# Small experts: the down projection in plain float32, with the unsplit weights as the stationary operand

## The chip, the cores and the metric

The kernel runs on one core of one Trainium2 chip. Its time is the device time of one execution in microseconds; runs are compared by their median. Besides the timed runs there is one execution taken with the hardware profiler; all rows below come from that.

## The reference

A two-layer encoder on 256 tokens of width 1024 in float32. Layer 0 ends in a dense SwiGLU, layer 1 in a mixture of eight SwiGLU experts of inner width 3584, of which each token uses two:

```python
logits = (t @ w_router).astype(jnp.float32)
top_v, top_i = lax.top_k(logits, TOP_K)
gates = jax.nn.softmax(top_v, axis=-1)
combine = jnp.sum(jax.nn.one_hot(top_i, N_EXPERTS) * gates[..., None], axis=1)
for e in range(N_EXPERTS):
    out = out + combine[:, e:e + 1] * (silu(t @ wg[e]) * (t @ wu[e])) @ wd[e]
```

Around it stand mixers, cross-attention and norms, which the change does not touch. The expert weights are 352 MB of float32, read once.

## The kernel before

**Numbers.** A float32 value is held as two parts of the type float32r, a rounded upper part and the rest, and a product is made of two or three matmuls of parts. Weights come from memory as float32 pieces of 1 MB (`raw`, 128 partitions of 2048 values). ACT copies the upper part (`wh`, L121, in two halves), DVE subtracts it for the lower part (`wl`, L123, whole piece), and PE multiplies by both. There are three buffers for `wh` and `wl`, and eleven for `raw`, taken in turn; a raw buffer is free for the next load when DVE has read it.

**Experts.** The loop runs over eight places; the experts are put into them by their number of tokens. Places 2, 4 and 7 (`SMALL`) have room for 64 tokens (`SCAP`), the others for 128. In a large place the tokens' upper and lower parts are separate tiles and a weight piece takes twelve matmuls (`mm3`). In a small place the 64 upper and the 64 lower columns stand side by side in one stationary tile of 128, and a piece takes eight matmuls of 512 columns (`mm2`, L994): four with `wh`, four with `wl`. The upper and lower halves of such a result are then added by the matmul that turns it.

**Chunks.** The inner width is cut into chunks of 1024, 1024, 1024 and 512. For a chunk, `gate_up` multiplies the tokens by eight pieces of gate and up weights (four for the last chunk) into `gu`. ACT scales the result out (`sgs`, L1026). `to_hT` turns it with PE: eight matmuls per 512 values, with `sgs` as the 128x128 plain-float32 weights and the 64 columns of `twice`, two stacked unit matrices, as the moving operand (L1047). ACT makes Silu of the gate part (L1049), DVE multiplies by the up part (L1050), and both split the product into upper and lower columns of `hs` (L129, L130). `hs` has two homes of one buffer each, the tags `hs` and `gain`, for the first and the second 512 values. `down` multiplies it by the pieces of down weights (four a chunk, two for the last) into two PSUM banks `y` that add up over the whole expert.

**Order.** The code asks for the down projection of a chunk after the gate and up of the next one: `gate_up(c)`, `down(c-1)`, `to_hT(c)`. The order of the instructions on each engine is fixed when the program is built; a scheduler moves them from the order of the code by its own estimate of when operands are ready. Each engine then works off its list strictly, and waits at an instruction whose operands or buffer are not ready. All weight loads are issued from SP's queue in the order of the code.

After the expert's last chunk the banks `y` are split (`split_y`), and `scatter` multiplies them by a one-hot matrix `st` and adds them to the rows of `x`. The last place's down projection stands behind the loop and is followed by the last norm (`finish`).

Of the kernel before, what the change touches and what calls it, by code (L numbers as in the profile page):

```python
# [55 lines left out]
def trunk_kernel(ctx: ExitStack, tc: tile.TileContext, io, out, stop=None):  # L56
# [716 lines left out]
    with ExitStack() as moe:  # L773
# [5 lines left out]
        def mbank(shape, name="mm"):  # L779
            return trp.tile(shape, F32, tag="tr", name=name)  # L780
# [133 lines left out]
        def slots(dst, t, e):  # L914

            at = byp[:, t, e:e + 1] if ids[1] is not None else pos[:, t, e:e + 1]
            chain["DVE"] = nc.vector.tensor_scalar(dst, iota2 if e in SMALL else iota, at, None, op0=OP.is_equal)

        def gained(kk, e, n, src):

# [34 lines left out]
        wg, wu, wd = io["moe_w_gate"][0], io["moe_w_up"][0], io["moe_w_down"][0]  # L955
        nch = len(CHUNKS)

        def one_hot(e):
            se = m2.tile([P, 2, P], F32, tag="sg", name="so", bufs=1)
            for t in range(2):  # L960
                slots(se[:, t, :], t, e)
            return se
# [8 lines left out]
            return rs  # L971

        def slots_T(e):
            se = one_hot(e)
            tp = mbank([P, 2, P], "setp")
# [3 lines left out]
            nc.scalar.activation(st, tp, AF.Copy)  # L979
            return st  # L980

        def gate_piece(w, e, c, i):

# [49 lines left out]

        def down_piece(e, c, i, parts=1):
            f0 = CHUNKS[c][0] + i * 256
            return load_w(wd[ids[e], f0:f0 + 256, :].rearrange("(k p) n -> p k n", p=P), 2, D, parts)

        def to_hT(e, sg, homes):
            hT = []
            for j, (pool, tag) in zip(range(sg.shape[-2]), homes):  # L1040
                hs = pool.tile([P, 2, 4, P], F32R, tag=tag, name="hs")
                if e in SMALL:

                    tp = mbank([P, 2, 4, SCAP], "htp")
# [3 lines left out]
                    h = m2.tile([P, 4, SCAP], F32, tag="hsm", name="hsm", bufs=1)
                    nc.scalar.activation(h, tp[:, 0, :, :], AF.Silu)  # L1049
                    nc.vector.tensor_tensor(h, h, tp[:, 1, :, :], op=OP.mult)  # L1050
                    hh = hs[:, 0, :, :]
                    chain["hh"], chain["hl"] = split_to(hh[:, :, 0:SCAP], hh[:, :, SCAP:P], h)
                    hT.append((hh, None))
                    continue
                tp = mbank([P, 4, P], "htp")
                for k in range(4):
                    nc.tensor.transpose(tp[:, k, :], sg[:, j, k * P:(k + 1) * P], ident)
                hh, hl = hs[:, 0, :, :], hs[:, 1, :, :]
                chain["hh"], chain["hl"] = split_to(hh, hl, tp)
                hT.append((hh, hl))  # L1060
            return hT

        def down(c, hT, yacc, i, w2):

            hh, hl = hT[i // 2]
            wh, wl = w2
            first, last = c == i == 0, c == nch - 1 and i == CHUNKS[c][1] // 256 - 1
            kn = [(i % 2 * 2 + k, k, n) for n in range(2) for k in range(2)]
            if hl is None:
                return mm2([(yacc[n], hh[:, kk, :], wh[:, k, n * 512:(n + 1) * 512], wl[:, k, n * 512:(n + 1) * 512])  # L1070
                            for kk, k, n in kn], first, last)
            return mm3([(yacc[n], hh[:, kk, :], hl[:, kk, :], wh[:, k, n * 512:(n + 1) * 512],
                         wl[:, k, n * 512:(n + 1) * 512]) for kk, k, n in kn], False, first, last)

        def split_y(yacc, n, pool=mA, tag="y"):
            y = pool.tile([P, 2, 512], F32R, tag=tag, name="y")
            split_to(y[:, 0, :], y[:, 1, :], yacc[n])
# [49 lines left out]
        twice = mA.tile([P, SCAP], F32, tag="twice", name="twice")  # L1127
        for i in range(2):
            nc.gpsimd.tensor_copy(twice[i * SCAP:(i + 1) * SCAP, :], ident[i * SCAP:(i + 1) * SCAP, i * SCAP:(i + 1) * SCAP])
        prev = y = st = nrs = pyacc = gf = None  # L1130
        for e in range(NE):
            for c in range(nch):
# [39 lines left out]
                        pyacc = nacc  # L1172
                        y = split_y(pyacc, 0)
                if c == 0:
                    yacc = [mmp.tile([P, 512], F32, tag="mm", name=f"y{n}") for n in range(2)]
# [133 lines left out]
```

## Time and profile before

| what | us |
|---|---|
| median of 3 runs (1668.41 to 1675.79) | 1669.49 |
| the profiled execution | 1665.06 |
| its span, first to last instruction | 1663.4 |
| expert loop, first gate/up matmul to the end | 638.7 to 1663.4 |

The span is the profiled part of the execution; 1.7 us lie around it. Each engine has its own line: PE is TensorE's matmuls, PEld its weight loads, DVE VectorE, ACT ScalarE, POOL GpSimd, SP the queue that issues the loads. A matmul's recorded duration overlaps the next one's, so PE's rate is read from starts. A plain-float32 matmul of the program is recorded as two matmuls and two weight loads; the type column says f32 for both kinds.

### The profile page before, as it was taken

What the parts mean: (1) busy time and instruction counts of PE and PEld (TensorE: products, weight loads), DVE (VectorE), ACT (ScalarE), POOL (GpSimd) and SP (SyncE); (2) the same over time, 40 slices, a digit from 0 to 9 for tenths busy, and PEclk for the clock granted to TensorE, in tenths of its full rate; (3) what the DMA queues carried; (4) which work ended last, traced back from release to release, by engine and by line L of the source; (5) the groups of instructions that cost most, each with busy time, mean ns of one, the idle gap of its engine ahead of it and who ended that gap; (6) DMA issues with size and microseconds to landing.
All of it is one profiled execution on the core that took longest, in us unless ns stands there. A gap on an engine that the chain in (4) does not pass through costs nothing. (4 is left out here: it accounts for less than half of the span.)

```text
span 1663.4 us, 22408 instructions
## 1 busy us (share of the span) xinstructions
PE 1572.4 (95%) x8448; PEld 1310.2 (79%) x8448; DVE 1262.8 (76%) x1214; ACT 1074.4 (65%) x1396; POOL 47.1 (3%) x75
## 2 busy tenths in 40 slices
PE   8999999999999999999999889999889999999885
PEld 7799889999989887888887667777667777777653
DVE  6785655445576657899988988978888978988876
ACT  6555554344554446787777787767777767677775
POOL 1010010000000102000000000000000000000000
PEclk9999999999999999999999999999999999999998
DMA  7456466565535586899999999999999999999980
GB/s 237 163 178 214 145 217 201 177 200 180 191 127 178 187 333 245 322 341 354 360 369 361 345 358 339 338 338 375 345 363 345 340 337 347 329 351 345 358 309 28
DMA packets 175409, 464.50 MB, mean 279 GB/s; under 512 B 9074, under 2 KB 64390, under 8 KB 175164
## 3 DMA queue, kind: packets, MB, share of 16 engines
q1 hardware_dynamic: 174412, 459.80, 77.0%
q0 software_dynamic: 880, 3.19, 0.6%
q8 instruction: 68, 1.11, 0.3%
q14 instruction: 49, 0.40, 0.1%
HBM read 461.90 MB, written 2.11 MB: 279 GB/s over the span
## 5 line engine op out<-in xcount | busy, mean ns | idle before, releaser
L123 DVE TENSOR_TENSOR wl<-raw,wh 128x2048 fp32r<-128x2048 f32 (+1 forms) x527 | 983.0, 1894 | 238.0 <-ACT wh L121 235.7
L121 ACT ACTIVATE wh<-raw 128x1024 fp32r<-128x1024 f32 x866 | 852.7, 1049 | 277.1 <-PE pws L141 92.0
L138 PE MATMUL gu<-wh,ch 128*128 128x512 f32 x560 | 221.3, 396 | 2.8 <-ACT sg L1030 2.8
L141 PE MATMUL gu<-wh,cl 128*128 128x512 f32 x560 | 219.7, 393 | 0.0
L144 PE MATMUL gu<-wl,ch 128*128 128x512 f32 x560 | 152.8, 395 | 10.6 <-DVE wl L123 10.5
L138 PE MATMUL pws<-nh,wh 128*128 128x256 f32 x560 | 137.5, 283 | 0.0
L141 PE MATMUL pws<-nl,wh 128*128 128x256 f32 x560 | 137.4, 283 | 0.0
L144 PEld LDWEIGHTS gu<-wl,ch 128*128 128x128 f32 x560 | 103.5, 188 | 40.3 <-DVE wl L123 19.1
L138 PEld LDWEIGHTS gu<-wh,ch 128*128 128x128 f32 x560 | 105.5, 188 | 27.1 <-ACT sg L1030 2.9
L994 PE MATMUL gu<-wl,ch 128*128 128x512 f32 x336 | 99.8, 419 | 24.5 <-DVE wl L123 23.5
L141 PEld LDWEIGHTS gu<-wh,cl 128*128 128x128 f32 x560 | 105.6, 189 | 21.8 <-DVE cl L1111 0.4
L141 PE MATMUL y<-wh,hs 128*128 128x512 f32 x280 | 110.9, 396 | 0.0
L138 PE MATMUL y<-wh,hs 128*128 128x512 f32 x280 | 110.4, 394 | 0.0
L138 PEld LDWEIGHTS pws<-nh,wh 128*128 128x128 f32 x560 | 106.2, 190 | 1.3 <-ACT wh L121 0.9
L141 PEld LDWEIGHTS pws<-nl,wh 128*128 128x128 f32 x560 | 106.0, 189 | 0.4
L994 PEld LDWEIGHTS gu<-wl,ch 128*128 128x128 f32 x336 | 59.0, 191 | 55.1 <-DVE wl L123 45.9
L994 PE MATMUL gu<-wh,ch 128*128 128x512 f32 x336 | 97.7, 405 | 4.4 <-ACT wh L121 4.3
L138 PE MATMUL acc<-wh,ch 128*128 128x512 f32 x216 | 84.7, 392 | 0.0
L141 PE MATMUL acc<-wh,cl 128*128 128x512 f32 x216 | 84.4, 391 | 0.0
L994 PEld LDWEIGHTS gu<-wh,ch 128*128 128x128 f32 x336 | 63.3, 192 | 24.1 <-ACT wh L121 10.8
L144 PE MATMUL y<-wl,hs 128*128 128x512 f32 x280 | 79.1, 404 | 2.0 <-DVE wl L123 2.0
L144 PE MATMUL pws<-nh,wl 128*128 128x256 f32 x560 | 78.9, 283 | 0.0
(363 smaller groups left out, 2182.2 us busy)
## 6 DMA issues: line engine op xcount, KB each, us to landing
raw<-in_moe_w_up_dram SPq DMA_DIRECT2D x112, 1024.0 KB, 6.5
raw<-in_moe_w_gate_dram SPq DMA_DIRECT2D x112, 1024.0 KB, 6.4
raw<-in_moe_w_down_dram SPq DMA_DIRECT2D x110, 1024.0 KB, 6.2
raw<-in_mem_w_kv_dram SPq DMA_DIRECT2D x16, 1024.0 KB, 5.5
raw<-in_odd_w_in_dram SPq DMA_DIRECT2D x12, 1024.0 KB, 5.3
raw<-in_ffn_w_gate_dram SPq DMA_DIRECT2D x11, 1024.0 KB, 5.1
raw<-in_ffn_w_up_dram SPq DMA_DIRECT2D x11, 1024.0 KB, 5.2
raw<-in_ffn_w_down_dram SPq DMA_DIRECT2D x11, 1024.0 KB, 4.7
```

The lines of the kernel that those rows point to most:

```text
L121: chain["wh"] = nc.scalar.activation(hf[:, sl], rf[:, sl], AF.Copy)
L123: chain["wl"] = nc.vector.tensor_sub(lf[:, sl], rf[:, sl], hf[:, sl].bitcast(F32))
L138: mm = nc.tensor.matmul(ps, ah, bh, start=f, stop=False, skip_group_check=bank)
L141: nc.tensor.matmul(ps, *((ah, bl) if w_left else (al, bh)), start=False, stop=False, skip_group_check=bank)
L144: mm = nc.tensor.matmul(ps, *((al, bh) if w_left else (ah, bl)), start=False, stop=e, skip_group_check=bank)
L994: mm = nc.tensor.matmul(ps, a, b[which], start=f, stop=e)
```

## The change

For the small places the weights of the down projection are no longer split: `down_piece` loads the raw piece alone, and `down` uses its 128x128 blocks as plain-float32 weights, with the hidden values as the 64 moving columns. The result is y transposed, eight blocks of 128 rows by 64 tokens in one PSUM bank. `to_hT` writes the hidden values as one float32 tile in the same two homes, without a split. `split_y` copies the bank once an expert (ACT, `yT`), turns it back with PE, four transposes for each half of the width, and splits that. One-hot tiles of a small place get 64 columns. Raw buffers of down pieces are now free when PE has used them.

```diff
         def down_piece(e, c, i, parts=1):
             f0 = CHUNKS[c][0] + i * 256
-            return load_w(wd[ids[e], f0:f0 + 256, :].rearrange("(k p) n -> p k n", p=P), 2, D, parts)
+            src = wd[ids[e], f0:f0 + 256, :].rearrange("(k p) n -> p k n", p=P)
+            return load_raw(src, 2, D) if e in SMALL else load_w(src, 2, D, parts)
...
-                    h = m2.tile([P, 4, SCAP], F32, tag="hsm", name="hsm", bufs=1)
+                    h = pool.tile([P, 4, SCAP], F32, tag=tag, name="h")
                     nc.scalar.activation(h, tp[:, 0, :, :], AF.Silu)
                     nc.vector.tensor_tensor(h, h, tp[:, 1, :, :], op=OP.mult)
-                    hh = hs[:, 0, :, :]
-                    chain["hh"], chain["hl"] = split_to(hh[:, :, 0:SCAP], hh[:, :, SCAP:P], h)
-                    hT.append((hh, None))
+                    hT.append(h)
...
+            first, last = c == i == 0, c == nch - 1 and i == CHUNKS[c][1] // 256 - 1
+            if type(yacc) is not list:
+                for d in range(KT):
+                    for k in range(2):
+                        mm = nc.tensor.matmul(yacc[:, d, :], w2[:, k, d * P:(d + 1) * P], hT[i // 2][:, i % 2 * 2 + k, :],
+                                              start=first and d == k == 0, stop=last and k == 1, skip_group_check=True)
+                return mm
...
+            if n == 0:
+                yT[0] = m2.tile([P, KT, SCAP], F32, tag="yT", name="yT", bufs=1)
+                nc.scalar.activation(yT[0], yacc, AF.Copy)
+            tp = mbank([SCAP, 4, P], "ytp")
+            for k in range(4):
+                nc.tensor.transpose(tp[:, k, :], yT[0][:, n * 4 + k, :], ident)
+            y = y[0:SCAP]
+            split_to(y[:, 0, :], y[:, 1, :], tp.rearrange("p a b -> p (a b)"))
```

The order on ACT in place 4, from the end of chunk 1's gate/up to the gate/up of chunk 2. Before: `sgs_10223` is chunk 1's result, `hsm` and `hs` its hidden values (10282 the first half, 10297 the second), `wh_10218`, `wh_10246` and `wh_10261` are down pieces, `wh_10316` and `wh_10331` the first gate pieces of chunk 2.

```order
L1026 ACTIVATE sgs_10223<-gu_10147,rs_9744 128x512
L1026 ACTIVATE sgs_10223<-gu_10148,rs_9744 128x512
L121 ACTIVATE wh_10218<-raw_10216 128x1024 x2
L1049 ACTIVATE hsm_10292<-htp_10283 128x256
L121 ACTIVATE wh_10246<-raw_10244 128x1024 x2
L129 ACTIVATE hs_10282<-hsm_10292 128x4x64
L121 ACTIVATE wh_10261<-raw_10259 128x1024 x2
L1049 ACTIVATE hsm_10307<-htp_10298 128x256
L121 ACTIVATE wh_10316<-raw_10314 128x1024 x2
L129 ACTIVATE hs_10297<-hsm_10307 128x4x64
L121 ACTIVATE wh_10331<-raw_10329 128x1024 x2
```

The same place of ACT's list now: `h_10328` and `h_10340` are the two halves of the hidden values, `wh_10347` and the following ones the gate pieces of chunk 2.

```order
L1027 ACTIVATE sgs_10238<-gu_10172,rs_9776 128x512
L1027 ACTIVATE sgs_10238<-gu_10173,rs_9776 128x512
L1050 ACTIVATE h_10328<-htp_10319 128x256
L1050 ACTIVATE h_10340<-htp_10331 128x256
L121 ACTIVATE wh_10347<-raw_10345 128x1024 x2
L121 ACTIVATE wh_10362<-raw_10360 128x1024 x2
L121 ACTIVATE wh_10377<-raw_10375 128x1024 x2
L121 ACTIVATE wh_10392<-raw_10390 128x1024 x2
L121 ACTIVATE wh_10417<-raw_10415 128x1024 x2
```

The splits of the down pieces are gone, and the second Silu stands ahead of the first gate piece of chunk 2, which stood ahead of the second `hs` before.

On PE, the down projection of chunk 0 at the same place, before: `hs_10044` is the first half of chunk 0's hidden values, the second follows below these rows.

```order
L1047 MATMUL htp_10283<-twice_6133,sgs_10223 128x64 x4
L1047 MATMUL htp_10298<-twice_6133,sgs_10223 128x64 x4
L994 MATMUL y0_10042<-wl_10212,hs_10044 128x512 x2
L994 MATMUL y1_10043<-wl_10212,hs_10044 128x512 x2
L994 MATMUL y0_10042<-wh_10218,hs_10044 128x512
L994 MATMUL y1_10043<-wh_10218,hs_10044 128x512
L994 MATMUL y0_10042<-wh_10218,hs_10044 128x512
L994 MATMUL y1_10043<-wh_10218,hs_10044 128x512
L994 MATMUL y0_10042<-wl_10219,hs_10044 128x512 x2
L994 MATMUL y1_10043<-wl_10219,hs_10044 128x512 x2
```

And now, from the last gate/up matmuls of chunk 1 (`gu_10172`, `gu_10173`): `h_10084` and `h_10096` are the halves of chunk 0's hidden values, in the two homes that `h_10328` and `h_10340` take over.

```order
L1070 MATMUL y_10074<-h_10084,raw_10234 128x64 x15
L995 MATMUL gu_10172<-wl_10222,ch_6101 128x512 x2
L995 MATMUL gu_10173<-wl_10222,ch_6101 128x512 x2
L1070 MATMUL y_10074<-h_10084,raw_10234 128x64
L1048 MATMUL htp_10319<-twice_6133,sgs_10238 128x64 x3
L1070 MATMUL y_10074<-h_10084,raw_10236 128x64 x16
L1048 MATMUL htp_10319<-twice_6133,sgs_10238 128x64 x4
L1048 MATMUL htp_10331<-twice_6133,sgs_10238 128x64 x7
L1070 MATMUL y_10074<-h_10096,raw_10275 128x64 x16
L1048 MATMUL htp_10331<-twice_6133,sgs_10238 128x64
L1070 MATMUL y_10074<-h_10096,raw_10293 128x64 x16
L995 MATMUL gu_10343<-wh_10347,ch_6101 128x512
```

The down matmuls read raw pieces, 16 to a piece, in unbroken runs between the turning ones; fifteen of them moved ahead of the last gate/up matmuls, and the first gate matmul of chunk 2 follows the last down matmul.

## Rows read from the trace of the kernel before

**Rows 1.** The page: busy time, share of the span and instructions of each engine.

```profile
PE 1572.4 (95%) x8448; PEld 1310.2 (79%) x8448; DVE 1262.8 (76%) x1214; ACT 1074.4 (65%) x1396; POOL 47.1 (3%) x75
```

**Rows 2.** Stretches: length, busy PE, PEld, DVE, ACT, POOL; clock, DMA share, GB/s.

```profile
1185.45:1219.44 33.99, 28.84 (x131) 20.79 (x129) 28.03 (x19) 26.91 (x34) 0.00 (x0) 1.00 0.96 345
1219.44:1243.24 23.80, 20.19 (x96) 15.01 (x95) 20.53 (x23) 18.03 (x24) 0.00 (x0) 1.00 1.00 372
1243.24:1280.19 36.95, 34.82 (x166) 28.13 (x165) 30.68 (x28) 31.66 (x40) 0.00 (x0) 1.00 0.93 347
1280.19:1312.68 32.49, 29.77 (x130) 23.22 (x129) 30.26 (x21) 22.74 (x27) 0.00 (x0) 1.00 0.92 329
1568.54:1602.51 33.97, 28.80 (x131) 20.80 (x129) 28.00 (x19) 26.92 (x34) 0.00 (x0) 1.00 0.81 292
1602.51:1630.61 28.10, 22.91 (x93) 16.00 (x92) 19.40 (x13) 19.53 (x25) 0.00 (x0) 0.94 0.65 246
...
932.82:1060.34 127.52, 113.68 (x520) 87.14 (x518) 109.08 (x88) 99.20 (x122) 0.00 (x0) 1.00 0.94 346
```

**Rows 3.** Groups by shape, 880 to 1660 us: count, busy us, mean ns, idle before.

```profile
L123 DVE TENSOR_TENSOR wl<-raw,wh 128x2048 fp32r<-128x2048 f32 x252 | 566.8, 2286 | 81.6 <-ACT wh L121 81.4 <-DMA raw<-in_moe_w_up_dram 0.2
L121 ACT ACTIVATE wh<-raw 128x1024 fp32r<-128x1024 f32 x502 | 489.8, 1053 | 6.1 <-PE gu L141 4.3 <-PE y L141 1.6
```

**Rows 4.** Timeline of DVE: start, length, instructions, idle before and who ended it.

```profile
1200.54 8.90 DVE L123 TENSOR_TENSOR wl<-raw,wh 128x2048 fp32r<-128x2048 f32 x4 [0.78 <-ACT wh L121]
```

**Rows 5.** Timeline of PE in expert 0, a large one, at PE's pace.

```profile
654.35 0.39 PE L141 MATMUL gu<-wh,cl 128*128 128x512 f32 x1
654.58 1.07 PE L144 MATMUL gu<-wl,ch 128*128 128x512 f32 x4
...
657.30 1.07 PE L144 MATMUL gu<-wl,ch 128*128 128x512 f32 x4
```

**Rows 6.** Waits of the queue that issues the loads: total us, times, longest.

```profile
SPq L106 <- DVE wl L123: 1127.6, 358, 17.1
```

**Rows 7.** Timeline of PE: turning the hidden values of expert 4.

```profile
1220.37 1.89 PE L1047 MATMUL htp<-twice,sgs 128*128 128x64 f32 x16
1222.07 1.18 PE L994 MATMUL y<-wl,hs 128*128 128x512 f32 x4
```

**Rows 8.** Timeline of PE: matmuls of the gather.

```profile
1241.13 0.28 PE L951 MATMUL xg<-sp,xh 128*128 128x256 f32 x1
1241.25 0.28 PE L952 MATMUL xg<-sp,xl 128*128 128x256 f32 x1
```

**Rows 9.** Timeline of all engines, last expert's last chunk and end.

```profile
1612.61 1.98 PE L1123 MATMUL gfp<-gfrow,ones 1*128 1x512 f32 x4
...
1617.63 6.70 DVE L123 TENSOR_TENSOR wl<-raw,wh 128x2048 fp32r<-128x2048 f32 x3 [1.00 <-ACT wh L121]
1617.65 0.73 PE L994 MATMUL gu<-wh,ch 128*128 128x512 f32 x2 [1.47 <-ACT wh L121]
1619.97 2.07 PE L994 MATMUL gu<-wl,ch 128*128 128x512 f32 x4 [1.60 <-DVE wl L123]
...
1647.02 1.09 ACT L129 ACTIVATE y<-y 128x512 fp32r<-128x512 f32 x2 [3.29 <-PE y L994]
```

**Rows 10.** Timeline of PE and ACT, expert 4: ACT waits for the down matmuls.

```profile
1196.94 1.21 PE L994 MATMUL y<-wl,hs 128*128 128x512 f32 x4 [0.61 <-DVE wl L123]
...
1198.19 0.42 ACT L129 ACTIVATE hs<-hsm 128x256 fp32r<-128x256 f32 x1 [1.47 <-PE y L994]
...
1232.28 0.42 ACT L129 ACTIVATE hs<-hsm 128x256 fp32r<-128x256 f32 x1 [1.45 <-PE y L994]
```

**Rows 11.** Timeline of PE: first gate matmuls of expert 5, chunks 0 and 1.

```profile
1256.35 0.39 PE L138 MATMUL gu<-wh,ch 128*128 128x512 f32 x1
...
1285.51 0.48 PE L138 MATMUL gu<-wh,ch 128*128 128x512 f32 x1
```

More of the change, by code (lines that the diff above doesn't have):

```diff
@@ L916, in slots @@
             at = byp[:, t, e:e + 1] if ids[1] is not None else pos[:, t, e:e + 1]
-            chain["DVE"] = nc.vector.tensor_scalar(dst, iota2 if e in SMALL else iota, at, None, op0=OP.is_equal)
+            chain["DVE"] = nc.vector.tensor_scalar(dst, (iota2 if e in SMALL else iota)[:, 0:dst.shape[-1]], at, None, op0=OP.is_equal)
         def gained(kk, e, n, src):
@@ L956, in trunk_kernel, with one_hot @@
         nch = len(CHUNKS)
-        def one_hot(e):
-            se = m2.tile([P, 2, P], F32, tag="sg", name="so", bufs=1)
+        def one_hot(e, m=P):
+            se = m2.tile([P, 2, m], F32, tag="sg", name="so", bufs=1)
             for t in range(2):
@@ L973, in slots_T @@
         def slots_T(e):
-            se = one_hot(e)
-            tp = mbank([P, 2, P], "setp")
+            m = SCAP if e in SMALL else P
+            se = one_hot(e, m)
+            tp = mbank([m, 2, P], "setp")
             for t in range(2):
@@ L978, in slots_T @@
             st = m2.tile([P, 2, P], F32R, tag="st", name="st", bufs=1)
-            nc.scalar.activation(st, tp, AF.Copy)
-            return st
+            nc.scalar.activation(st[0:m], tp, AF.Copy)
+            return st[0:m]
         def gate_piece(w, e, c, i):
@@ L1047, in to_hT @@
                             nc.tensor.matmul(tp[:, i, k, :], sg[:, i, j, k * P:(k + 1) * P], twice, start=True, stop=True)
[L1048 removed]
+                    h = pool.tile([P, 4, SCAP], F32, tag=tag, name="h")
                     nc.scalar.activation(h, tp[:, 0, :, :], AF.Silu)
                     nc.vector.tensor_tensor(h, h, tp[:, 1, :, :], op=OP.mult)
[L1051 to L1053 removed]
+                    hT.append(h)
                     continue
+                hs = pool.tile([P, 2, 4, P], F32R, tag=tag, name="hs")
                 tp = mbank([P, 4, P], "htp")
@@ L1063, in down @@
         def down(c, hT, yacc, i, w2):
+            first, last = c == i == 0, c == nch - 1 and i == CHUNKS[c][1] // 256 - 1
[5 more added lines that the diff above has]
+                return mm
             hh, hl = hT[i // 2]
             wh, wl = w2
-            first, last = c == i == 0, c == nch - 1 and i == CHUNKS[c][1] // 256 - 1
             kn = [(i % 2 * 2 + k, k, n) for n in range(2) for k in range(2)]
-            if hl is None:
-                return mm2([(yacc[n], hh[:, kk, :], wh[:, k, n * 512:(n + 1) * 512], wl[:, k, n * 512:(n + 1) * 512])
-                            for kk, k, n in kn], first, last)
             return mm3([(yacc[n], hh[:, kk, :], hl[:, kk, :], wh[:, k, n * 512:(n + 1) * 512],
@@ L1076, in split_y @@
             y = pool.tile([P, 2, 512], F32R, tag=tag, name="y")
-            split_to(y[:, 0, :], y[:, 1, :], yacc[n])
+            if type(yacc) is list:
+                split_to(y[:, 0, :], y[:, 1, :], yacc[n])
+                return y
+            if n == 0:
[6 more added lines that the diff above has]
+            split_to(y[:, 0, :], y[:, 1, :], tp.rearrange("p a b -> p (a b)"))
             return y
@@ L1129, in trunk_kernel @@
             nc.gpsimd.tensor_copy(twice[i * SCAP:(i + 1) * SCAP, :], ident[i * SCAP:(i + 1) * SCAP, i * SCAP:(i + 1) * SCAP])
+        yT = [None]
         prev = y = st = nrs = pyacc = gf = None
@@ L1174, in trunk_kernel @@
                 if c == 0:
-                    yacc = [mmp.tile([P, 512], F32, tag="mm", name=f"y{n}") for n in range(2)]
+                    if e in SMALL:
+                        yacc = mmp.tile([P, KT, SCAP], F32, tag="mm", name="y")
+                    else:
+                        yacc = [mmp.tile([P, 512], F32, tag="mm", name=f"y{n}") for n in range(2)]
                 hT = to_hT(e, sg, ((mA, "hs"), (pA, "gain")))
@@ L1200, in trunk_kernel @@
         pe, pc, hT, yacc = prev
-        with behind("hh", "hl"):
-            w2 = [down_piece(pe, pc, i, 2) for i in range(2)]
+        w2 = [down_piece(pe, pc, i) for i in range(2)]
         for i in range(2):
```

1 line of the change is left out of this document (removed).

## The prediction

> **What bounds the kernel now.** I read the busy times first: PE 95%, DVE 76%, ACT 65% of the span [rows 1]. PE's figure says little, since a 512-column matmul is recorded as 0.39 us while the next one starts 0.23 us later [rows 5], so the reader should go on to the busy time by stretch. The expert loop is cut there at the start of the last gate/up matmul of each chunk [rows 2]. In each cut lie the down projection of the chunk before, the turning of the hidden values, and the gate/up of the next chunk. For expert 4 (small) the four stretches in which a small expert's down weights are used take 33.99 (A, chunk 1 to 2), 23.80 (B, 2 to 3), 36.95 (C, 3 to chunk 0 of the next expert, a large one) and 32.49 us (D), together 127.23; the same four of expert 2 are 127.52. In A, DVE is busy 28.03 of 33.99 and ACT 26.91: both split all twelve weight pieces, at 2.29 us a piece on DVE and two of 1.05 us on ACT [rows 3]. DVE back to back does four pieces in 8.90 us, 2.2 each [rows 4]. So A and B go at the pace of the splits, with PE short of work; C and D, with a large expert's twelve matmuls a piece, go at PE's pace: 2.72 us a piece [rows 5]. Transfers are behind neither: the loads' queue waits 1127.6 us in total for DVE to release a raw buffer [rows 6].
>
> **What goes.** For 42 pieces (three small experts, 14 each) the split goes: about 96 us of DVE and 88 us of ACT by [rows 3], and the split of h. Of that only what PE waits for is worth anything.
>
> **What comes on PE.** A down piece was 8 matmuls of 512 columns, at 0.23 us 1.86 us. It becomes 16 plain-float32 matmuls with 128x128 weights and 64 moving columns. The trace has just this form: turning h multiplies 128x128 float32 by the 64 columns of `twice`. The eight matmuls of the program stand there as 16 records, from 1220.37 to 1222.07: 1.70 us, 0.2125 each [rows 7]. So a piece costs 16 x 0.2125 = 3.40 us, +1.54, and 14 pieces +21.6 us an expert. From below, a split-float32 matmul of 256 columns with one weight load takes 0.12 us [rows 8], so 1.9 a piece; from above, four matmuls at the half clock took 2.07 us [rows 9] where 1.07 is usual [rows 5], so about 6.6. I take 0.2125, since that row is the same form, and keep the ends for the rivals.
>
> **What moves: the wait ahead of the next splits.** hT has two homes, one buffer each. The Silu that writes the second half of the new h must wait until PE has finished the last two pieces of the old down projection. Before, the queue of ACT had the split of the first gate piece ahead of the write that waits for this (`hs`); now the Silu stands ahead of all of them, and all gate pieces queue behind it on ACT, and behind ACT the lower halves on DVE and then PE. That such a wait is real is shown by [rows 10]: ACT sat idle 1.47 us until the down matmuls ended (the last four started at 1196.94, so their slots end at 1197.87) and went on at 1198.19. From there to the last gate/up matmul of A (1219.44) are 21.25 us, in B from 1232.28 to 1243.24 10.96 us.
>
> *A.* From the start of the last gate/up matmul: its slot 0.23; PE's rest of the down pieces and turning, as the new order has it: 1+16+16+16 down matmuls and 15 turning ones, 64 x 0.2125 = 13.6; 0.3 until ACT goes on (the lag in rows 10); then the 21.25 of before, plus one more piece split in this stretch, 2.2, since the first gate piece is no longer done in advance. Ten down matmuls of the next pieces stand before the last four gate/up matmuls (2.1 us; some 0.2 of it in PE's wait): 1.9. Sum 39.5, +5.5.
> *B.* Six left of the first piece, 48 more and 8 turning: 62 x 0.2125 = 13.2; 0.23 + 13.2 + 0.3 + 10.96 + 2.2 = 26.9, +3.1.
> *C.* PE alone: 64 down and 8 turning matmuls, 15.3, and the gather's 2.5 (some 21 matmuls at 0.12, rows 8) give 18.0 to the first gate matmul of the large expert; before it came after 13.1 (1256.35, [rows 11]). The half piece split ahead feeds it 0.9 us; Silu (0.4) and the other half (1.0) begin 0.3 after the turning, DVE's first lower half ends at 22.1, PE's first piece at 23.0; seven pieces of 2.72 and four down matmuls (0.85) make 42.9, less the slot of 0.23 42.7: +5.7.
> *D.* 28 down matmuls, 5.95, then y^T: 0.3 + 0.6 for ACT's copy, 0.6 for four transposes. The large expert's first matmul started 5.3 us in ([rows 11], 1285.51) and will start at about 7.7; ACT's splits there began late anyway, so I count +1.8. The second four transposes, in the next stretch: +0.3.
> Experts 2 and 4: 5.5 + 3.1 + 5.7 + 1.8 + 0.3 = 16.4 each.
> *Expert 7.* A as above, 33.97 before: +5.5. B (28.10 before): 13.4 to the end of the down pieces, two 512-column matmuls for the last gain and their copies, about 3 with Silu (the pair took 1.98, [rows 9]), ACT's split 2.0, then the 12.98 of before from DVE's 1617.63 to 1630.61: 31.4; part of that 12.98 was PE on the half clock, so +3 rather than +3.3. End: 5.4 pieces x 3.40 + 0.85 turning = 19.1, copy, transposes and waits 1.7, against 16.4 before (from 1630.61, where the last stretch of [rows 2] ends, to ACT's 1647.02, [rows 9]): +4.5; then the second half of y must be transposed after the first scatter rather than lie ready (transposes 0.3, split 0.6, wait 0.6): +1.5. Together +14.5.
> Sum: 2 x 16.4 + 14.5 = +47.3. Small edits (one-hots of 64 columns, the missing split of h: 0.8 us on ACT and DVE per half) lie beside ACT's and DVE's new idle time: nothing. The stretch from chunk 0 to 1 of each small expert keeps a large expert's down pieces: nothing.
> The profiled execution took 1665.06 (span 1663.4 and 1.7 around it): 1712. The median of the runs lies 4.4 above it, so 1669.5 + 47 = 1716; I say 1715. The stretch's own range is 1700 to 1728.
>
> **Rivals.**
> 1. *The stalls go altogether.* ACT and DVE have so much time now that PE never waits: A = 14.9 gate/up + 13.6 + 3.4 = 31.9, B 26.3, C 39.9, D 32.7, which is 130.8 for 127.2, +3.6; expert 7 about +1. Sum +8: 1677, just no change. For it: DVE is the busiest in A and loses 11 of its 28 us. Against it: the order on ACT puts the Silu first. The Trainium skill, "Perfetto Trace Analysis", section "Identifying the Most-Contended Engine", says to take DVE and ACT by occupancy and TensorE by weight-load time. By that rule the load on DVE, 82% in A, is what to relieve and A could fall to 32; the trace agrees that DVE is busiest there (28.03 against 20.79 of weight loads), but its waits are on ACT, and ACT's on PE.
> 2. *All of PE's work is added.* If nothing of today's waiting is given back, it is 42 x 1.54 = +65: 1734. For it: C, D and the end run at PE's pace; against: A holds 33.99 - (14.9 + 7.5 + 3.4) = 8 us of PE waits.
> 3. *The clock falls in the down stage.* The granted clock falls to the lower of its two levels, 1.2 GHz, after stretches in which PE did little: two matmuls between waits of 1.47 and 1.60 us, and the four behind them took 2.07 us instead of 1.07 [rows 5, 9]; the mean granted clock of that stretch is 0.94 [rows 2]. If a run of 64-column matmuls counts as little, the down stage doubles, 14 x 3.4 = 48 us an expert, 143 more: 1858. Against it: the turning matmuls run at the full 2.4 GHz, though for 1.7 us only. The Trainium skill, "TensorE: Matmul & The Clock Gate", section "Part 1: The HAM clock gate", has the low clock as the default and activity as what lifts it; if thin matmuls were too little activity, the time would be that of this rival, and no row here has a long run of them.
> 4. *The other side: a matmul costs less in a long run.* If the second weight load of a plain-float32 matmul hides in runs of 16 (at 0.12, rows 8), a down piece costs 1.9 and the 224 matmuls of an expert 20.7 less: 16.4 - 20.7 = -4.3 twice and 14.5 - 20.7 = -6.2: -15, 1655. It decides from below about 0.14 us a matmul. Against it: the turning runs are 8 long and show no such thing.
>
> **How the numbers follow.** Forecast 0.68, rival 1 0.12, rival 2 0.10, rival 3 0.04, rival 4 0.06. The range takes the forecast's own spread, most of rival 2 and the way towards rival 1: 1684 to 1736. What a measurement here can tell from no change is 0.5%, 8.3 us. Slower: the forecast, 2, 3 and half of 1, 0.87; same: the other half of 1 and a little of 4, 0.07; faster: 4, 0.06.
>
> **What would show it.** In the new profile: 224 plain-float32 down matmuls per small expert as 448 records, 0.106 us apart in runs of 32; ACT's Silu waiting about 8 us a stretch for PE's y; behind it PE waiting for ACT and DVE, one piece each 2.2 us; A near 39, B 27, C 42.6, D 34; DVE's busy time down by about 100 us. Wrong if the records stand 0.06 or 0.2 us apart, if splits run during the down stage, or if the granted clock is 0.5 in it.

## The result, and the profile after

The changed kernel takes 1740.69 us (median of four runs, 1738.13 to 1746.35) against 1671.17 for the kernel before beside it: a ratio of 1.0433, interval 1.0405 to 1.0461, slower by some 70 us. The forecast was 1715 with a range of 1684 to 1736: the direction and the mechanism came out, the size did not, and the time lies above the range. One execution in what follows, the profiled one of experiment 10 (2051.38 us), had a mean granted clock of 0.742 and is left out of that experiment's median.

The page of the new profile, answering to [rows 1], and its groups by shape (count, busy us, mean ns, idle before):

```profile
PE 1660.1 (95%) x9480; PEld 1415.5 (81%) x9480; DVE 1164.9 (67%) x1149; ACT 990.6 (57%) x1290; POOL 46.7 (3%) x75
...
L1070 PEld LDWEIGHTS y<-h,raw 128*128 128x128 f32 x1344 | 154.3, 192 | 1.3
L1070 PE MATMUL y<-h,raw 128*128 128x64 f32 x1344 | 155.4, 274 | 0.0
L1051 DVE TENSOR_TENSOR h<-h,htp 128x256 f32<-128x256 f32 x21 | 8.5, 418 | 119.9 <-ACT h L1050 119.9
L1050 ACT ACTIVATE h<-htp 128x256 f32<-128x256 f32 x21 | 7.7, 384 | 102.7 <-PE htp L1048 54.1 <-PE y L1070 48.6
```

DVE lost 98 us of work and ACT 84, PE gained 88. Part of what was taken from DVE and ACT came back as waiting: DVE stands 119.9 us before the 21 multiplications that make h, because ACT's Silu does, and 48.6 us of the Silu's 102.7 are for PE's down matmuls.

The stretches, cut as in [rows 2] at the start of each chunk's last gate/up matmul: A to D of expert 4, then A, B and the end of expert 7 (length; busy PE, PEld, DVE, ACT, POOL; clock, DMA share, GB/s).

```profile
1215.00:1255.80 40.80, 37.22 (x232) 31.83 (x231) 19.14 (x12) 18.82 (x24) 0.00 (x0) 0.92 0.86 306
1255.80:1284.91 29.11, 26.38 (x173) 23.33 (x172) 12.08 (x17) 10.77 (x15) 0.00 (x0) 0.88 0.81 285
1284.91:1329.32 44.41, 42.19 (x270) 37.05 (x269) 21.84 (x23) 20.54 (x27) 0.00 (x0) 1.00 0.80 283
1329.32:1365.64 36.32, 34.45 (x178) 26.81 (x176) 25.23 (x18) 24.23 (x29) 0.00 (x0) 1.00 0.83 292
1623.81:1664.99 41.18, 37.33 (x232) 32.02 (x230) 19.14 (x12) 18.82 (x24) 0.00 (x0) 0.92 0.72 249
1664.99:1698.52 33.53, 30.79 (x189) 25.95 (x188) 9.83 (x6) 11.44 (x15) 0.00 (x0) 0.85 0.52 183
1698.52:1739.40 40.88, 25.94 (x198) 22.92 (x196) 6.71 (x13) 7.07 (x15) 3.60 (x4) 0.80 0.07 28
```

A is 6.8 us longer, B 5.3, C 7.5 and D 3.8, and the clock of A and B, 1.00 before, is 0.92 and 0.88. One restart (PE's first gate/up matmuls behind a down stage) shows why: the timeline of the new kernel at the end of A's down stage, PE, ACT and DVE (start, length, what, idle before and who ended it).

```profile
1216.07 3.74 PE L1070 MATMUL y<-h,raw 128*128 128x64 f32 x32
1219.64 2.62 PE L1048 MATMUL htp<-twice,sgs 128*128 128x64 f32 x22
...
1225.89 3.74 PE L1070 MATMUL y<-h,raw 128*128 128x64 f32 x32
...
1229.67 0.38 ACT L1050 ACTIVATE h<-htp 128x256 f32<-128x256 f32 x1 [8.55 <-PE y L1070]
1229.95 7.67 ACT L121 ACTIVATE wh<-raw 128x1024 fp32r<-128x1024 f32 x8
...
1231.05 2.16 PE L995 MATMUL gu<-wh,ch 128*128 128x512 f32 x4 [1.42 <-ACT wh L121]
...
1231.97 8.89 DVE L123 TENSOR_TENSOR wl<-raw,wh 128x2048 fp32r<-128x2048 f32 x4 [1.47 <-ACT wh L121]
...
1234.32 2.07 PE L995 MATMUL gu<-wl,ch 128*128 128x512 f32 x4 [1.11 <-DVE wl L123]
```

The Silu waits 8.55 us until the last y matmul has been worked off, and the split of the first gate piece stands behind it. So PE ends the down stage with nothing prepared (called a cold restart below), waits 1.42 us for the upper half, 1.11 us for the lower. And the matmuls behind the second gap run at 2.07 us for four, twice the 1.07 of [rows 5]. The windows of this kernel say the same: clock 1.00 through the down stage and the first gap, 0.50 for the 6.83 us that follow.

```profile
1215.00:1231.30 16.30, 14.88 (x131) 14.70 (x130) 1.26 (x4) 3.24 (x6) 0.00 (x0) 1.00 0.76 245
1231.30:1238.13 6.83, 5.72 (x13) 3.59 (x13) 6.16 (x3) 6.32 (x7) 0.00 (x0) 0.50 0.68 268
```

### The profile page after: what moved, and what is told of

Same layout as the page of the kernel before. It is cut to its first block, busy times and chain, and to the rows that moved or that the text cites. A ratio compares the mean times of both kernels' runs of the same rounds, so it can differ in the third digit from the quotient of the medians.

```text
span 1739.4 us, 24206 instructions
## 1 busy us (share of the span) xinstructions
PE 1660.1 (95%) x9480; PEld 1415.5 (81%) x9480; DVE 1164.9 (67%) x1149; ACT 990.6 (57%) x1290; POOL 46.7 (3%) x75
## 5 line engine op out<-in xcount | busy, mean ns | idle before, releaser
L123 DVE TENSOR_TENSOR wl<-raw,wh 128x2048 fp32r<-128x2048 f32 (+1 forms) x483 | 887.1, 1867 | 241.0 <-ACT wh L121 237.8
L121 ACT ACTIVATE wh<-raw 128x1024 fp32r<-128x1024 f32 x778 | 768.1, 1052 | 277.0 <-PE pws L141 99.2
L138 PE MATMUL gu<-wh,ch 128*128 128x512 f32 x560 | 221.6, 396 | 3.8 <-ACT sg L1031 2.8
L144 PE MATMUL gu<-wl,ch 128*128 128x512 f32 x560 | 154.2, 396 | 11.6 <-DVE wl L123 11.5
L1070 PEld LDWEIGHTS y<-h,raw 128*128 128x128 f32 x1344 | 154.3, 192 | 1.3
L1070 PE MATMUL y<-h,raw 128*128 128x64 f32 x1344 | 155.4, 274 | 0.0
L144 PEld LDWEIGHTS gu<-wl,ch 128*128 128x128 f32 x560 | 102.8, 188 | 41.9 <-DVE wl L123 20.8
L138 PEld LDWEIGHTS gu<-wh,ch 128*128 128x128 f32 x560 | 105.3, 188 | 28.7 <-ACT wh L121 4.3
L995 PE MATMUL gu<-wl,ch 128*128 128x512 f32 x336 | 105.9, 440 | 19.0 <-DVE wl L123 18.1
L995 PE MATMUL gu<-wh,ch 128*128 128x512 f32 x336 | 106.7, 436 | 12.0 <-ACT wh L121 11.8
L995 PEld LDWEIGHTS gu<-wl,ch 128*128 128x128 f32 x336 | 65.6, 209 | 47.1 <-DVE wl L123 35.2
L995 PEld LDWEIGHTS gu<-wh,ch 128*128 128x128 f32 x336 | 67.5, 207 | 33.9 <-ACT wh L121 19.9
L1051 DVE TENSOR_TENSOR h<-h,htp 128x256 f32<-128x256 f32 x21 | 8.5, 418 | 119.9 <-ACT h L1050 119.9
```

Of the source, the lines that this page charges most:

```text
L121: chain["wh"] = nc.scalar.activation(hf[:, sl], rf[:, sl], AF.Copy)
L123: chain["wl"] = nc.vector.tensor_sub(lf[:, sl], rf[:, sl], hf[:, sl].bitcast(F32))
L138: mm = nc.tensor.matmul(ps, ah, bh, start=f, stop=False, skip_group_check=bank)
L144: mm = nc.tensor.matmul(ps, *((al, bh) if w_left else (ah, bl)), start=False, stop=e, skip_group_check=bank)
L995: mm = nc.tensor.matmul(ps, a, b[which], start=f, stop=e)
L1070: mm = nc.tensor.matmul(yacc[:, d, :], w2[:, k, d * P:(d + 1) * P], hT[i // 2][:, i % 2 * 2 + k, :], start=first and d == k == 0, stop=las ...
```

## The experiments

The first question: is the extra 70 us PE's longer matmuls, or the cold restart behind them? Two theories on the clock go with it: it falls because of the waits (Q), or because of thin matmuls, those of 64 columns (T). The stretches of expert 4 in us; each kernel's median and its ratio to the kernel before, measured beside it, stand with its experiment.

| kernel | A | B | C | D |
|---|---|---|---|---|
| before | 33.99 | 23.80 | 36.95 | 32.49 |
| after | 40.80 | 29.11 | 44.41 | 36.32 |
| 1, second homes | 36.38 | 23.08 | 44.42 | 36.32 |
| 2, wide | 38.07 | 24.81 | 40.38 | 32.26 |
| 3, half the down matmuls | 33.76 | 22.83 | 36.45 | 33.64 |
| 5, wide with the wait | 42.34 | 29.98 | 41.52 | 31.16 |
| 11, gaps filled | 39.95 | 27.35 | 44.42 | 36.35 |
| 4, before with second homes | 32.25 | 22.07 | 37.01 | 32.45 |
| 7, 4 with half the change | 32.44 | 22.90 | 39.10 | 31.66 |
| 9, 4 with six plain pieces | 31.87 | 22.33 | 36.99 | 31.86 |

**1. Second homes for h.** Nothing but the Silu's wait for old down pieces goes.

```diff
-                    h = pool.tile([P, 4, SCAP], F32, tag=tag, name="h")
+                    h = pool.tile([P, 4, SCAP], F32, tag=tag, name="h", bufs=1)
...
-                hT = to_hT(e, sg, ((mA, "hs"), (pA, "gain")))
+                hT = to_hT(e, sg, ((m2, "h0"), (m2, "h1")) if e in SMALL and c % 2 == 0 else ((mA, "hs"), (pA, "gain")))
```

> The changed kernel, with homes of their own for the small experts' h tiles of every even chunk, so that the second Silu of a down stage no longer waits for the last two old down pieces; nothing else is changed. Theory Q (ACT's queue: the added time is the thin down matmuls plus a cold restart that the Silu's wait causes): the gate pieces are split while PE is in the down stage, the first gate/up matmul follows the last y matmul at once. PE's own work in stretch A of expert 4 is then the bound: gate/up 64 x 0.268 = 17.1, 64 down matmuls x 0.223 = 14.3, 16 htp x 0.2125 = 3.4, sum 34.8 us against 40.8 measured; B 26.3 against 29.1; C 41.7 against 44.4. The whole kernel about 1708 us (1700 to 1715). If PE's clock still falls behind the down stage (Theory T: it falls because of the thin matmuls in the down stage, not because of the waits behind it), the waits go but 6.8 us at half clock stay in each restart: A about 38, whole about 1722. Rival P (PE's added work alone, waits were there before as well and are hidden): no change, 1737 to 1744.

Measured: 1714.05 us, ratio 1.0276 (1.0236 to 1.0315). The same place in this kernel, ACT and PE:

```profile
1211.98 3.74 PE L1070 MATMUL y<-h,raw 128*128 128x64 f32 x32
1212.18 0.38 ACT L1050 ACTIVATE h<-htp 128x256 f32<-128x256 f32 x1 [4.98 <-PE htp L1048]
...
1212.46 4.83 ACT L121 ACTIVATE wh<-raw 128x1024 fp32r<-128x1024 f32 x5
...
1215.53 1.18 PE L995 MATMUL gu<-wh,ch 128*128 128x512 f32 x4
```

ACT goes on 3 us before the down stage ends, and PE passes from y to gate/up without a gap. The clock is 1.00 in A and B of expert 4:

```profile
1201.09:1237.47 36.38, 34.99 (x232) 30.08 (x231) 19.14 (x12) 18.71 (x24) 0.00 (x0) 1.00 0.87 325
1237.47:1260.55 23.08, 23.08 (x174) 21.72 (x173) 12.09 (x17) 10.89 (x15) 0.00 (x0) 1.00 0.89 329
```

So the cold restart is worth 4.4 us in A, 6.0 in B and 26.6 in the whole (difference of the medians). In B, PE is busy throughout and the stretch is shorter than before the change, although its down pieces are longer. One cold restart is left, that of B in expert 7, only 1.2 us shorter than after. Its gaps stand as they were, and 6.83 us at clock 0.50 with them:

```profile
1652.13 2.16 PE L995 MATMUL gu<-wh,ch 128*128 128x512 f32 x4 [1.63 <-ACT wh L121]
1655.41 2.07 PE L995 MATMUL gu<-wl,ch 128*128 128x512 f32 x4 [1.11 <-DVE wl L123]
```

C stays: there the Silu waits 10.10 us for the turning, as in the changed kernel, and not for a home. Theory Q's time, 1708, was a little low; it gave C 2.7 us back. T and the rival P fall for A and B.

**2. The raw weights as the moving tile.** h stationary, four matmuls of 512 columns a piece, y by tokens, no yT.

```diff
...
-                for d in range(KT):
+                for n in range(2):
                     for k in range(2):
-                        mm = nc.tensor.matmul(yacc[:, d, :], w2[:, k, d * P:(d + 1) * P], hT[i // 2][:, i % 2 * 2 + k, :],
+                        mm = nc.tensor.matmul(yacc[n][0:SCAP, :], hT[i // 2][:, i % 2 * 2 + k, :], w2[:, k, n * 512:(n + 1) * 512],
...
```

> The changed kernel with its plain float32 down matmuls turned round: h (64 columns) is the stationary tile and the raw weights move, 512 columns at a time, into y by tokens; so 4 matmuls a piece in place of 16, no yT and no transposing back. The Silu's wait stays as it is. Theory T (thin matmuls let the clock fall): the clock stays at 1.0 behind the down stage; 8 restarts get back about 3.4 us each. Theory Q (the waits at the restart let it fall): the stretches of 6.8 us at clock 0.5 stay. For the length of a piece both leave open 3.4 us (four passes of 512 columns each for 4 matmuls: 16 x 0.2125) as in the changed kernel. The yT chain's part in D (3.8 us a small expert, 5 at the end by my reading) goes: about 1725 under Q, about 1700 under T; 1740 if a piece costs the same and neither the yT chain nor the clock counted.

Measured: 1692.30 us, ratio 1.0147 (1.0107 to 1.0188), better than either theory allowed. PE's timeline in A:

```profile
1193.38 12.23 PE L1070 MATMUL y<-raw,h 128*64 128x512 f32 x28
1205.54 3.56 PE L1048 MATMUL htp<-twice,sgs 128*128 128x64 f32 x30
1208.91 1.18 PE L995 MATMUL gu<-wh,ch 128*128 128x512 f32 x4
```

28 records (3.5 pieces) take 12.16 us from start to start, 3.47 a piece: no cheaper to speak of than 3.57. There is no gap, and the clock stays up. But this tells Q and T not apart: with the other lengths the scheduler put the first gate piece ahead of the Silu, so the waits went together with the thin matmuls. C and D are 4 us shorter than after, and PE is never short of work there:

```profile
1255.93:1296.31 40.38, 40.38 (x166) 26.51 (x164) 22.19 (x23) 22.82 (x29) 0.00 (x0) 1.00 0.88 326
1296.31:1328.57 32.26, 32.26 (x129) 21.86 (x127) 26.03 (x19) 21.08 (x25) 0.00 (x0) 1.00 0.85 323
```

In C the two kernels differ in the order on ACT. In both the Silu waits for the turning, which PE does behind its down matmuls; in the changed kernel half a piece is split ahead of that Silu, here two and a half. C of the changed kernel, then of this one:

```profile
1292.58 1.06 ACT L121 ACTIVATE wh<-raw 128x1024 fp32r<-128x1024 f32 x1
1303.74 0.38 ACT L1050 ACTIVATE h<-htp 128x256 f32<-128x256 f32 x1 [10.10 <-PE htp L1048]
```

```profile
1263.16 4.84 ACT L121 ACTIVATE wh<-raw 128x1024 fp32r<-128x1024 f32 x5
1274.87 0.39 ACT L1050 ACTIVATE h<-htp 128x256 f32<-128x256 f32 x1 [6.88 <-PE htp L1048]
```

**3. Half of the down matmuls.** The second 128 rows of each down piece are left out of the result.

```diff
-                    for k in range(2):
+                    for k in range(1):
                         mm = nc.tensor.matmul(yacc[:, d, :], w2[:, k, d * P:(d + 1) * P], hT[i // 2][:, i % 2 * 2 + k, :],
...
```

> The changed kernel with only the first of the two 128-row halves of each down piece multiplied (8 plain float32 matmuls a piece in place of 16): half of the small experts' down projection is left out of the result. 42 pieces are shorter by 8 x 0.223 = 1.78 us, 75 us in all. Theory 'the down stage is on the path one to one, and the restart is cold whatever its length': 1740 - 75 = 1665, A of expert 4 33.7, and the stretches at clock 0.5 still there. Theory T (the clock falls because the thin matmuls go on for 14 us): the dips go as well, 1640 to 1650. Theory 'ACT and DVE bound the stretch, PE's time is partly hidden': less than 40 us gained, 1700 or more.

Measured: 1670.50 us, ratio 1.0008 (0.9982 to 1.0035): 70 us won of the 75 taken out. A, B and C shorten by 7.0, 6.3 and 8.0 for four pieces of 1.78 (7.1), D by 2.7 for two. The down stage is on the path one to one, also at the cold restart, where the clock still falls: A's mean is 0.90 with half as many thin matmuls.

**4. The kernel before, with second homes.** The same edit on `hs`.

```diff
-                hs = pool.tile([P, 2, 4, P], F32R, tag=tag, name="hs")
+                hs = pool.tile([P, 1 if pool is m2 else 2, 4, P], F32R, tag=tag, name="hs", bufs=1)
...
```

> The kernel before, with homes of their own for the small experts' split h (hs) of every even chunk, so that ACT no longer waits for old down matmuls before it writes hs (1.45 us each in Rows 10). Theory: ACT and DVE bound the small experts' stretches before the change, so most of these waits come back: 1650 to 1662. Rival: PE or the pieces' own pace bounds them, the waits are slack: 1668 to 1673, no change.

Measured: 1658.48 us, ratio 0.9938 (0.9912 to 0.9964), faster by 10 us: A and B of expert 4 lose 1.7 us each, where the waits of [rows 10] were 1.47 and 1.45. The theory holds.

**5. The wide kernel with the wait put back.** ACT's first gate split is issued behind the Silu.

```diff
+                    if e in SMALL and c and i == 0 and not res:
+                        late.append("h")
                     wh, wl = ready.pop(0) if ready else gate_piece(w, e, c, i)
+                    late.clear()
...
+                  with behind(*late):
                     chain["wh"] = nc.scalar.activation(hf[:, sl], rf[:, sl], AF.Copy)
...
```

> The kernel of e2_wide (raw weights as the moving tile, 512 columns) with one thing forced: ACT splits the first gate piece of chunks 1 to 3 of a small expert only after the second Silu of the chunk before, as the changed kernel's order has it. In e2_wide the new order of ACT's queue put that piece ahead of the Silu, so that kernel took away the thin matmuls and the waits together. Theory T' (the clock falls only where thin matmuls and waits come together): the waits of 1.4 and 1.1 us at the restart are back, the clock stays at 1.0 in the small experts; 6 places (A and B of three experts) cost 2.5 to 4 us each: 1707 to 1716. Theory Q (the wait alone lets the clock fall): six stretches of 3.4 to 6.8 us at clock 0.5, another 1.7 to 3.4 us each: 1718 to 1736. Rival R (the wait in front of the restart costs nothing, e2_wide is faster by its matmuls alone): 1690 to 1695.

Measured: 1722.75 us, ratio 1.0320 (1.0288 to 1.0352), in the band of theory Q. The restart in A, PE alone, and the windows of A and B:

```profile
1226.95 0.74 PE L998 MATMUL gu<-wh,ch 128*128 128x512 f32 x2 [1.42 <-ACT wh L124]
...
1230.22 2.07 PE L998 MATMUL gu<-wl,ch 128*128 128x512 f32 x4 [1.59 <-DVE wl L126]
```

```profile
1209.48:1251.82 42.34, 38.34 (x146) 23.13 (x144) 19.15 (x12) 18.95 (x24) 0.00 (x0) 0.92 0.84 297
1251.82:1281.80 29.98, 26.75 (x84) 14.00 (x83) 11.21 (x13) 9.56 (x12) 0.00 (x0) 0.89 0.81 284
```

The gaps are back and with them six stretches of 6.83 us at clock 0.5, one at each restart of A and B, behind down matmuls of 512 columns. Thin down matmuls are not needed for the clock to fall.

**6. The wide kernel with second homes too.** The edits of 1 and 2 together.

> The kernel of e2_wide with the homes of e1_homes as well; ACT's order is that of e2_wide, only the Silu's wait for old down pieces goes. In e2_wide ACT has one gate piece split when the down stage ends and A is 38.07 us; with the wait gone four are split, as in e1_homes (A 36.4). Theory (the wait still costs): A 36.4, B 23.1, sum of six stretches 3 x (1.7 + 1.7) = 10 us, about 1682. Rival (one piece split ahead is cover enough): 1689 to 1695.

Measured: 1694.28 us, ratio 1.0160 (1.0127 to 1.0193), as 2, in the rival's range. But it does not decide between the two: the homes take away a wait that no longer bound. In 2 the Silu waits for the turning, and here it waits just as long, with the same one piece split ahead. The first Silu of A in 2, then here:

```profile
1207.35 0.38 ACT L1050 ACTIVATE h<-htp 128x256 f32<-128x256 f32 x1 [11.17 <-PE htp L1048]
```

```profile
1208.17 0.38 ACT L1050 ACTIVATE h<-htp 128x256 f32<-128x256 f32 x1 [11.18 <-PE htp L1048]
```

Whether four pieces split ahead would be worth more than one in this form is not shown.

**7. The kernel of 4 with two of four down pieces plain float32**, in the form of 2.

```diff
+            return load_raw(src, 2, D) if e in SMALL and i > 1 else load_w(src, 2, D, parts)
...
```

> The kernel of e4_before_homes with half of the change: in the small experts the down pieces of the second 512 rows of a chunk (2 of 4) are plain float32, h the stationary tile and the raw weights moving, into the same accumulators (rows 0 to 63); the others stay split in two. PE's work in A rises by 2 x 1.7 us from 27.9 to 31.3, ACT's falls by 2 x 2.1 and DVE's by 2 x 2.3. Theory B (PE's time and the splits both count, whichever is larger in a stretch): A and B stay within 1 us of e4_before_homes (32.25, 22.07), whole 1650 to 1662. Theory 'PE counts one to one': 18 pieces x 1.7 = +31, 1688. Theory 'ACT and DVE bound': 18 x 2.1 = -38, 1620.

Measured: 1666.65 us, ratio 0.9986 (0.9970 to 1.0002), 8 us above 4. A is 0.2 longer with 4.5 us less work on DVE and, by the count above, 3.4 more on PE; B is 0.8 longer, C 2.1 longer. Neither engine's load alone sets the time; theory B is nearest, some 5 us too low: it left out C. Transfers are no rival here, though the DMA engines are busy 0.92 to 1.01 of A and B in 4, 7 and 9: no wait in these stretches ends on a transfer in 4, one of 0.3 us in 7, and one each of 0.3 and 0.4 in 9.

**8. No turn of y.** The small experts' rows are added unturned.

```diff
...
-            split_to(y[:, 0, :], y[:, 1, :], tp.rearrange("p a b -> p (a b)"))
+            split_to(y[:, 0, :], y[:, 1, :], yacc[0:SCAP].rearrange("p a b -> p (a b)"))
```

> The changed kernel without the turn of y: no yT, no transposes back, y is split straight from the first 64 rows of its bank, so the small experts' rows that are added to x are left wrong and their summing up is left out. This isolates one term of the prediction, the yT chain (D +1.8 an expert by the sum, +1.5 at the end). Theory (the whole +3.9 of D and 2 of the +8.1 at the end are this chain): D of expert 4 falls from 36.3 to 32.4, as in e2_wide, 2 x 3.9 + 2 to 3 = about 10 us, whole 1728 to 1732. Rival (D's excess is the down stage and its restart; e2_wide won it by its order): D stays over 35, whole 1736 to 1741.

Measured: 1736.57 us (1728.78 to 1745.22), ratio 1.0421 (1.0388 to 1.0455), not distinguishable from the changed kernel. D falls by 0.9 us only:

```profile
1322.39:1357.83 35.44, 32.60 (x172) 26.52 (x170) 26.59 (x20) 23.32 (x27) 0.00 (x0) 1.00 0.83 300
```

My reading of D's excess was wrong, the rival's right: it is the two longer down pieces (2 x 1.7). The waits for split pieces, 1.71 and 1.13 us, are no longer than before (32.49 less 29.77 of busy PE):

```profile
1331.57 0.50 PE L138 MATMUL gu<-wh,ch 128*128 128x512 f32 x1 [1.71 <-ACT wh L121]
...
1334.84 1.19 PE L144 MATMUL gu<-wl,ch 128*128 128x512 f32 x4 [1.13 <-DVE wl L123]
```

In 2, without these waits, D with pieces as long takes 32.26. And the clock stays at 1.00 in D over these two gaps: waits of this size do not lower it everywhere.

**9. The kernel of 4 with one piece in four plain, in chunks 0 and 1 only** (second homes in the odd chunks).

```diff
+            return load_raw(src, 2, D) if e in SMALL and i == 3 and c in (0, 1) else load_w(src, 2, D, parts)
...
```

> The kernel before with the homes of e4_before_homes (here those of every odd chunk) and one down piece in four plain float32 (h stationary, raw weights moving), in chunks 0 and 1 of the small experts alone: 6 pieces in all. PE's work in A is then 27.9 + 1.7 = 29.6 us, in B 21.1; e4_before_homes took 32.25 and 22.07 there. Theory (in those two stretches ACT and DVE bound e4_before_homes, PE has room): A 30.5, B 21.6, about 1650 to 1655. Rival (the restart behind the down stage, not the splits, holds the difference to PE's work): A and B as in e4_before_homes or 1 us longer, 1658 to 1666.

Measured: 1654.88 us, ratio 0.9918 (0.9899 to 0.9937): faster than both kernels, like 4, and from 4 not to be told by these intervals. A is 0.4 shorter than in 4, B 0.3 longer, as the rival had it; that the time still fell into the theory's range proves nothing for it.

**10 and 11. The gaps filled.** Matmuls that feed nothing, 7 behind the last y matmul and 5 behind the first four gate/up matmuls, at the restarts of A and B.

```diff
+            with behind(after):
+                ps = mbank([P, 512], "warm")
+                for _ in range(n):
+                    nc.tensor.matmul(ps, xgh[:, 0, :], xgh[:, 0:4, :], start=True, stop=True)
...
```

> The changed kernel with matmuls that feed nothing in the gaps of the restart: at the six places where chunk 2 or 3 of a small expert begins, 7 matmuls of 512 columns behind the last y matmul (some 1.6 us, where PE waited 1.4 us for wh) and 5 behind the first four gate/up matmuls (some 1.1 us, where it waited 1.1 us for wl). The waits for the split pieces stay, PE only stands idle no longer. Theory Q (the idle time lets the clock fall): the stretches of 6.8 us at clock 0.5 behind the down stages go; each gives back up to 3.4 us and the fill costs up to 0.5 us: A of expert 4 from 40.8 to 37.5 or 38.5, B from 29.1 to 26 or 27, the whole 1720 to 1730. Theory S (the late splits themselves hold the stretch, the clock falls in time that PE would wait anyway): the clock stays up and A and B hardly move, 1736 to 1742. Theory T (thin matmuls alone let it fall): the clock still falls, 1740 to 1744.

> The kernel of e10_fill once more, for a trace at the full clock level (the profiled execution of e10_fill ran at clock 0.742 throughout, which can't be set against the others). Its timed runs had a mean granted clock of 0.984 to 0.991 (0.977 in the changed kernel), so theories S and Q alike expect the stretches of 6.8 us at clock 0.5 behind the down stages gone. Theory Q: A of expert 4 37.5 to 38.5, B 26 to 27. Theory S: A and B over 40 and 28.5, and the time came from elsewhere.

Measured: 10 took 1730.08 us (median of four), ratio 1.0343 (1.0303 to 1.0384); 11, the same kernel, 1728.62, ratio 1.0336 (1.0273 to 1.0400). Of 11, the restart of A on PE, and A and B:

```profile
1225.73 1.87 PE L993 MATMUL warm<-ch 128*128 128x512 f32 x7
1227.43 0.65 PE L1003 MATMUL gu<-wh,ch 128*128 128x512 f32 x2
...
1228.86 1.31 PE L993 MATMUL warm<-ch 128*128 128x512 f32 x5
1230.62 1.20 PE L1003 MATMUL gu<-wl,ch 128*128 128x512 f32 x4 [0.44 <-DVE wl L123]
```

```profile
1211.29:1251.24 39.95, 38.06 (x243) 32.18 (x242) 19.14 (x12) 18.72 (x24) 0.00 (x0) 1.00 0.87 307
1251.24:1278.59 27.35, 26.69 (x186) 23.58 (x184) 12.00 (x17) 10.80 (x15) 0.00 (x0) 1.00 0.83 281
```

Behind the same thin matmuls and the same late splits the clock stays at 1.00 once these gaps are filled, at all six restarts. That gives back 0.85 us in A and 1.76 in B, 9.6 over the six: between theories Q and S. It is what is left after the fill's own cost; the first fill takes 1.70 us where the gap was 1.42. The half clock is the smaller part of the restart's 26.6; the larger part is the waiting for pieces that could have been split earlier (2 splits its first one at 1194.18, 14.7 us before its restart).

## Why the prediction was wrong in size

The mechanism was read rightly from the order and the trace: the Silu at the head of ACT's queue, its wait of 8 us (8.55), ACT and DVE idle through the down stage, a piece more to split behind it, DVE's load down by about 100 us, a full clock in the down stage. Rival 3, the clock falling in that stage, did not come: 1.00 there. Rival 1 did not come either, and 1 shows that its A (31.9) was too low: even without the gap at the restart the stretch takes 36.38. Rival 4 fell with the pace.

What failed is the sum. The profiled executions differ by 76.0 us of span (1739.4 less 1663.4), the steps gave 47.3. The 28.7 between, by steps:

- *The pace, "a piece costs 16 x 0.2125 = 3.40 us".* A run of 32 records goes from 1216.07 to 1219.64: 3.57 a piece, 0.223 a matmul. The row it was taken from has 16 records and takes 1.70 us [rows 7]. The trace of before had the right pace as well, 34 us earlier in the same expert: 16 records of the same form in 1.81 us, 0.226 a matmul (shown behind this list). The difference makes 42 x 0.17 = 7.1 us, spread over all stretches.
- *The restart, "one more piece split in this stretch, 2.2"* (A and B). The waits were priced, the clock behind them was not, although [rows 9] showed the pattern with its half-clock group at the one place where it happened before. 11 puts 9.6 us to it, net of the fill. With the pace, A came out 40.80 for 39.5 and B 29.11 for 26.9; over the three experts 4.7 and 7.0 us beyond the sum.
- *C +5.7 and D +1.8* came out at +7.5 and +3.8 for expert 4, for the two experts 7.3 beyond the sum. D's term said that ACT's splits began late anyway and would cover the longer down pieces. They began late, but as late as before: of D's 3.83 us, 0.88 is the turn of y, by 8, and the other 2.95 stand against 2 x 1.71 of added PE work. 2, with down pieces nearly as long, no turn of y and no waits for split pieces, has C and D 4 us shorter each. How C's excess divides between pace and late pieces is not separated.
- *"The stretch from chunk 0 to 1 ... nothing"*: +2.0, +0.6 and +1.9, together 4.5 us. 15 of the new y matmuls stand ahead of its last gate/up matmuls, and the sum counts them in no stretch. Besides, a half-clock stretch of 3.41 us lies in it for experts 2 and 7; before, there was one for expert 4. PE's gap there is 1.36 us each time, and the clock fell behind it or did not: that part is luck.
- *The end, +4.5 and +1.5*: 40.9 for 32.8, 2.1 beyond it.
- What is left, 2.9 us, lies ahead of the expert loop, where nothing was changed: 1.7 of it is one half-clock stretch of 6.83 us in place of 3.41. The excesses of the stretches, 4.7, 7.0, 7.3, 4.5, 2.1, 0.2 (the second four transposes) and this, make the 28.7; the 7.1 of the pace and the 9.6 of the clock are causes within them.

The longer run of 16 records in the trace of before, from 1186.16 to 1187.97:

```profile
1186.16 2.00 PE L1047 MATMUL htp<-twice,sgs 128*128 128x64 f32 x16
1187.97 1.18 PE L994 MATMUL y<-wl,hs 128*128 128x512 f32 x4
```

Seen as a balance: PE's added work is 42 x (3.57 - 1.86) = 72 us, which is nearly the whole result, as in rival 2 with the right pace (1741). That is a coincidence of two terms. 1 is 45 us slower than before, so some 27 of the 72 are given back, by this difference, where ACT and DVE no longer hold PE up; the restart of the changed kernel takes 26.6 away again. My forecast had PE's 65 with 18 given back on balance; it was nothing on balance.

The rule of the Trainium skill, "Perfetto Trace Analysis", section "Identifying the Most-Contended Engine", would have had the relief of DVE shorten A. Measured, DVE fell from 28.03 to 19.14 us in A and A grew from 33.99 to 40.80; but PE's work grew along with it, so this does not refute the rule. In 7 DVE fell from 27.84 to 23.38 against 4, PE gained some 3.4, and A stayed: the relief paid for PE's work there. What occupancy did not show is what stood at the head of ACT's queue, and that is worth 4.4 of A's 6.8 us, by 1. The same skill's "TensorE: Matmul & The Clock Gate", section "Part 1: The HAM clock gate", has activity lift the clock; the runs agree in the direction: full through 14 us of thin matmuls, down right behind a gap of 1.42 us, full where the gap was filled. A gap alone does not settle it: with 1.71 and 1.13 us in D of 8 the clock stayed at 1.00.

## What to carry to other kernels

Work that is moved from a helper engine to PE costs its full time where the stage stands on PE's path (3); where it fills PE's waits for the helper it can cost nothing (9: six pieces, some 10 us more on PE, and no longer than 4). What is saved on the helper counts only if that engine can use the time: look in its in-order queue for a write that waits for PE, and give its tile a second buffer before anything else (26.6 us in the changed kernel, 10 in the one before). A second buffer helps only where the write waits for that buffer last (not in 6). Price a restart behind such a wait with the clock, not only with the pieces that are late. Take the pace of an instruction from more than one run, the longest above all.

## What the runs showed of the hardware

Plain float32 costs nearly the same whichever operand stands: 16 matmuls of 64 columns with 128x128 weights take 3.57 us a piece, four of 512 columns with 64 stationary columns 3.47, where the eight float32r matmuls of 512 columns took 1.86. The y matmuls stand back to back: 1344 records at a distance of 0.112 us are 150 us, and the weight loads' 154.3 lie beside them. In the changed kernel and in 5, PE's gaps of 1.4 to 1.6 us and 1.1 to 1.6 us at a restart went with 6.83 us at half the clock (10.24 in B of expert 7 of the changed kernel) at all six restarts of A and B, behind thin and wide matmuls alike; in 1 and 11, whose thin matmuls run as long without these gaps, A and B of expert 4 stand at 1.00, and in B of expert 7 in 1, where the gaps of 1.63 and 1.11 us are left, so is the half clock. Elsewhere gaps of this size went either way: behind 1.36 us from chunk 0 to 1 the clock fell once in three before and twice in three after, and behind 1.71 and 1.13 us in D of 8 not at all. What tells these cases apart is open.
